# Split weights in padded buffers at set byte distances from the activations, on a two-layer hybrid trunk

## The chip, the cores and the metric

The program runs on one core of a Trainium2 chip. The metric is device time in microseconds, the median of several runs; lower is better. TensorE (PE in the profile; PEld is its weight load), VectorE (DVE), ScalarE (ACT) and GpSimd (POOL) each work through their own instructions in order and wait for each other by semaphores; SyncE (SP) issues most DMAs.

## The reference

A residual stream x of 256 tokens by 2048 passes through two layers in float32. Each layer normalizes x, multiplies it by one wide input matrix, runs two groups of heads, gates them, and multiplies the result by an output matrix that is added to x.

```python
def layer_ab(x, norm_g, w_in, ...):
    h = rms_norm(x, norm_g)
    proj = jnp.einsum('btd,de->bte', h, w_in)
    q, k, v, o_pre, z_a, i_pre, f_pre, z_b, xbc, dt_raw = split_cols(proj, SPLIT_AB)
    y_a = mlstm_branch(...)
    y_b = mamba2_branch(...)
    y = jnp.concatenate([y_a, y_b], axis=-1).astype(x.dtype)
    return x + jnp.einsum('bte,ed->btd', y, w_out)

def layer_cd(x, norm_g, w_in, kv_norm, w_uk, w_uv, ...):
    h = rms_norm(x, norm_g)
    proj = jnp.einsum('btd,de->bte', h, w_in)
    q_c, ckv, z_c, iq, ik, iw, qkv, z_d, b_pre, a_pre = split_cols(proj, SPLIT_CD)
    y_c = dsa_branch(...)
    y_d = gdn_branch(...)
    y = jnp.concatenate([y_c, y_d], axis=-1).astype(x.dtype)
    return x + jnp.einsum('bte,ed->btd', y, w_out)
```

The mixers are an mLSTM, a Mamba-2 SSD, a top-k sparse attention and a gated DeltaNet. Most of the arithmetic lies in the projections by w_in (2048 x 13352 and 2048 x 18064) and w_out (4096 x 2048 and 6144 x 2048).

## The kernel before

**Projections.** float32 is kept by splitting each operand into a high part and a remainder, both of type fp32r, and adding three products: high by high, high by low, low by high. The activations are split once, into hT (the normalized input, 16 blocks of 128 features; each block has 256 columns of high parts and 256 of low parts), into cT (the latent of the sparse attention) and into the units ua, ub and uc (the gated outputs that go into w_out). The weights come by DMA through `load_w` (lines 198 to 212) in groups of 128 x 2048 into wr (three buffers). ScalarE copies wr to wh (the high part, line 210), VectorE subtracts wh from wr to make wl (line 211). wh and wl have two buffers each.

Two helpers use them:

- `proj_tok` (token projection, PSUM tile pt) loads 128 x 128 of the activations into TensorE and moves 512 columns of wh or wl through it.
- `proj_feat` (feature projection, PSUM tile pf) loads 128 x 128 of wh or wl and moves 256 columns of the activations through it.

Every matmul is issued at line 75, transposes at line 79. The order on each engine is set by a scheduler from the order of the code; between the matmuls of a projection, `tick` (line 184) takes one step of the mixers' generators. TensorE's order is the program's.

**Where the tiles lie.** In the built program each tile starts at these bytes of its partition, modulo 256; blocks and column slices inside the tiles are multiples of 512 bytes apart and don't change them:

| tile | start modulo 256 |
|---|---|
| hT | 192 |
| wh, wl (all buffers) | 160 |
| ua, ub, uc | 160 |
| cT | 32 |

So the moving operand's start minus the loaded operand's, modulo 256, is:

| projection | moving | loaded | distance |
|---|---|---|---|
| token, on hT | wh, wl | hT | 224 |
| token, on ua, ub, uc | wh, wl | ua, ub, uc | 0 |
| token, on cT | wh, wl | cT | 128 |
| feature, on hT | hT | wh, wl | 32 |
| feature, on cT | cT | wh, wl | 128 |

**Other places that the change touches.** `tri` (line 103) is a 128 x 256 tile of ones whose left half becomes the upper triangle; `ones` (line 106) is a tile of its own, used in the matmuls den, rbp and gcT. In the gated DeltaNet, `norms` (line 1191) and `delta` (line 1308) square tiles on ScalarE only for the sum of a row (accum_out); the squares themselves go into the scratch tile gjunk. Before that stage the gates of layer cd are computed: 12 token projections in a row, while VectorE steps through a triangular solve (`solve`, U) and GpSimd finishes it (lines 1029 to 1034).

```python
PE.matmul(pts[t][:, :n], hi, wh[:, k % KG, :n], start=k == 0, stop=False)
PE.matmul(pt, wh[:, k, bs], xt[:, i, 0:256], start=g + k == 0 and b % 2 == 0, stop=False)
```

In these two lines, of the token and of the feature projection, the operand named second is loaded and the one named third moves.

Of the kernel before, what the change touches and what calls it, by code (L numbers as in the profile page):

```python
# [8 lines left out]
F32 = mybir.dt.float32  # L9
F32R = mybir.dt.float32r  # L10
I32 = mybir.dt.int32
AF = mybir.ActivationFunctionType
# [15 lines left out]
GONE = -3.4e38  # L28

KG, WR, WS = 4, 3, 2  # L30

STEPS = 1150

# [29 lines left out]
def trunk(ctx, tc, x, rel_bias, ab_norm, ab_w_in, ab_ml_b_i, ab_ml_b_f, ab_ml_norm, ab_ssm_conv_w,  # L63
# [4 lines left out]
    V, A, G = nc.vector, nc.scalar, nc.gpsimd  # L68
    ticking = []

    class PE:
# [5 lines left out]
        @staticmethod  # L77
        def transpose(*args, **kw):
            return held(nc.tensor.transpose(*args, **kw))  # L79
# [9 lines left out]
    cp = ctx.enter_context(tc.tile_pool(name="cp", bufs=1))  # L89
    wp = ctx.enter_context(tc.tile_pool(name="wp", bufs=3))  # L90
# [12 lines left out]
    tri = cp.tile([128, 256], F32, name="tri")  # L103
    V.memset(tri, 1.0)
    G.affine_select(tri[:, 0:128], tri[:, 0:128], pattern=[[1, 128]], compare_op=OP.is_ge, fill=0.0, base=0, channel_multiplier=-1)
    ones = cp.tile([128, 128], F32, name="ones")
    V.memset(ones, 1.0)

    def mx(name):
        return ps.tile([128, 512], F32, name=name, tag="mx")  # L110
# [45 lines left out]
    def pump():  # L156

        for gen in list(bg):
            if next(gen, "end") == "end":
                bg.remove(gen)  # L160
# [11 lines left out]
    def scaled_to(n):  # L172

        while scaling["done"] < n:
            next(scaling["gen"], None)
            scaling["done"] += 1

    def tick():

        if scaling["wait"] is not None and scaling["done"] < 8:  # L180
            scaling["wait"] -= 1
            if scaling["wait"] <= 0:
                scaled_to(scaling["done"] + 1)
                scaling["wait"] = 2
        ticking.append(True)
        if steps and next(steps[0], "end") == "end":
            steps.pop(0)
        ticking.clear()

    def lag(n):  # L190
        for _ in range(n):
            yield
# [2 lines left out]
        while steps:  # L195
            tick()

    def load_w(src, r0, nk, pieces, n):

        pump()  # L200
        shaped = lambda w: w.rearrange("p k n -> p (k n)").rearrange("p (k n) -> p k n", n=n)
        wr = shaped(wp.tile([128, KG, 512], F32, name="wr", tag="wr", bufs=WR))
        if sum(m for _, m, _ in pieces) < n:
            G.memset(wr[:, 0:nk, 0:n], 0.0)
        for c0, m, at in pieces:
            nc.sync.dma_start(wr[:, 0:nk, at:at + m], src[r0:r0 + nk * 128, c0:c0 + m].rearrange("(k p) n -> p k n", p=128))
        wh = shaped(wp.tile([128, KG, 512], F32R, name="wh", tag="wh", bufs=WS))
        wl = shaped(wp.tile([128, KG, 512], F32R, name="wl", tag="wl", bufs=WS))
        with tc.high_priority():
            A.copy(wh[:, 0:nk, 0:n], wr[:, 0:nk, 0:n])  # L210
            V.tensor_tensor(wl[:, 0:nk, 0:n], wr[:, 0:nk, 0:n], wh[:, 0:nk, 0:n].bitcast(F32), op=OP.subtract)  # L211
        return wh, wl

    def proj_tok(src, r0, X, c0, n=512, apart=False):

        pts = [ps.tile([128, 512], F32, name=f"pt{t}", tag="pt") for t in range(2)]
        nk = len(X)

        def part(w, k, t):
            (wh, wl), (xt, i) = w, X[k]  # L220
            hi, lo = xt[:, i, t * 128:t * 128 + 128], xt[:, i, 256 + t * 128:384 + t * 128]
            PE.matmul(pts[t][:, :n], hi, wh[:, k % KG, :n], start=k == 0, stop=False)
            PE.matmul(pts[t][:, :n], hi, wl[:, k % KG, :n], start=False, stop=False)
            PE.matmul(pts[t][:, :n], lo, wh[:, k % KG, :n], start=False, stop=k == nk - 1)

        if apart:

            w = [load_w(src, r0 + g * 128, KG, [(c0, n, 0)], n) for g in range(0, nk, KG)]
            for t in range(2):
                for k in range(nk):  # L230
                    part(w[k // KG], k, t)
                    tick()
            return pts
        for g in range(0, nk, KG):
            w = load_w(src, r0 + g * 128, KG, [(c0, n, 0)], n)
            if g + KG == nk:
                order = [(k, t) for t in range(2) for k in range(KG)]
            else:
                order = [(k, t) for k in range(KG) for t in range(2)]
            for i, (k, t) in enumerate(order):  # L240
                part(w, g + k, t)
                if i % 2:
                    tick()
        return pts

    def proj_feat(src, r0, X, pieces, groups=None, raw=False):

        n = max(p[2] + p[1] for p in pieces)
        n = (n + 127) // 128 * 128
        nb = n // 128  # L250
        pts = [ps.tile([128, 512], F32, name=f"pf{b}", tag="pt") for b in range((nb + 1) // 2)]
        nk = len(X)
        kg = KG * 512 // n
        for g, m in groups or [(g, min(kg, nk - g)) for g in range(0, nk, kg)]:
            wh, wl = load_w(src, r0 + g * 128, m, pieces, n)
            last = g + m == nk
            order = [(k, b) for b in range(nb) for k in range(m)] if last else [(k, b) for k in range(m) for b in range(nb)]
            for at, (k, b) in enumerate(order):
                xt, i = X[g + k]
                if xt is hT and not raw:  # L260
                    scaled_to(i // 2 + 1)
                bs = slice(b * 128, b * 128 + 128)
                pt = pts[b // 2][:, b % 2 * 256:b % 2 * 256 + 256]
                PE.matmul(pt, wh[:, k, bs], xt[:, i, 0:256], start=g + k == 0 and b % 2 == 0, stop=False)
                PE.matmul(pt, wh[:, k, bs], xt[:, i, 256:512], start=False, stop=False)
                PE.matmul(pt, wl[:, k, bs], xt[:, i, 0:256], start=False, stop=last and k == m - 1 and (b % 2 == 1 or b == nb - 1))
                if at % nb == nb - 1:
                    tick()
        return pts
# [164 lines left out]
    with ExitStack() as st:  # L434
        mp = st.enter_context(tc.tile_pool(name="mp", bufs=1))
        np1 = ExitStack()
        X, rb = normed(gab, np1.enter_context(tc.tile_pool(name="np1", bufs=1)), True, 9)
# [48 lines left out]
        pt = mx("RTp")  # L486
# [27 lines left out]
        for i in range(8):  # L514
            k = 1 << i
# [10 lines left out]
        pt = mx("R2Tp")  # L526
# [115 lines left out]
        with tc.tile_pool(name="lp", bufs=1) as lp:  # L642
# [71 lines left out]
            pt = mx("rbp")  # L714
# [10 lines left out]
            for h in range(4):  # L725
# [7 lines left out]
                v = lp.tile([128, 2, 512], F32, name="v", tag="v", bufs=2)  # L733
# [32 lines left out]
    with ExitStack() as st:  # L766
# [3 lines left out]
        X, rb = normed(gcol[:, G_CD:G_CD + 16], kq, False, 6)  # L770
# [185 lines left out]
        pt = mx("rkp")  # L956
# [202 lines left out]
        with tc.tile_pool(name="gp", bufs=1) as gp:  # L1159
# [14 lines left out]
            for i in range(4):  # L1174
                pts = proj_feat(cd_w_in, 0, X, [(CQKV + i * 512, 512, 0)])
                qc = gp.tile([128, 4, 256], F32, name="qc", tag="qc", bufs=QB)
                ssq = gp.tile([128, 2, 4], F32, name="ssq", tag="ssq", bufs=2)
                junk = gp.tile([128, 128], F32, name="gjunk", tag="gjunk")
                for b in range(2):
                    conv_gate(pts[b], gconv, i * 4 + b * 2, 64, None, qc[:, b * 2:b * 2 + 2].rearrange("p b t -> p (b t)"))  # L1180
                rq = gp.tile([128, 8], F32, name="rq", tag="rq", bufs=2)
# [2 lines left out]
                def norms(qc, ssq, rq, rq2):  # L1184
                    yield from lag(LQ)
                    for j in range(4):
                        pt = mx("qt")
                        for t in range(2):
                            transpose(pt[:, t * 128:t * 128 + 128], qc[:, j, t * 128:t * 128 + 128])
                        for t in range(2):  # L1190
                            A.activation(junk, pt[:, t * 128:t * 128 + 128], AF.Square, scale=0.5, accum_out=ssq[:, t, j:j + 1])
                        yield

                    rsqrt(rq, ssq.rearrange("p t j -> p (t j)"), 1.0)
                    V.tensor_scalar(rq, rq, scalar1=0.5 * 128 ** -0.5, scalar2=None, op0=OP.mult)
                    V.tensor_tensor(rq2, rq, rq, op=OP.mult)

                steps.append(norms(qc, ssq, rq, rq2))
                for s in range(2):
                    h0, j0 = i * 8 + s * 4, i * 4 + s * 2  # L1200
# [46 lines left out]
                    o = gp.tile([128, 2, 512], F32, name="og_", tag="og_")  # L1247
                    z = gp.tile([128, 2, 512], F32, name="zg", tag="zg")

                    def delta(s, h0, qc, kT, k0, QD, Wt, vf, o, z, rq, rq2):  # L1250
                        hsl = [slice(h * 128, h * 128 + 128) for h in range(4)]
                        v = gp.tile([128, 2, 512], F32, name="vg", tag="vg")
# [12 lines left out]
                        for c in range(2):  # L1265
# [16 lines left out]
                            u = gp.tile([128, 512], F32, name="u", tag="u")  # L1282
# [22 lines left out]
                        sso = gp.tile([128, 8], F32, name="sso", tag="sso", bufs=2)  # L1305
                        for c in range(2):
                            for h in range(4):
                                A.activation(junk, o[:, c, hsl[h]], AF.Square, accum_out=sso[:, c * 4 + h:c * 4 + h + 1])

                        dup = lambda r: r.rearrange("p (c j) -> p c j", c=2)[:, :, s * 2:s * 2 + 2].unsqueeze(3).to_broadcast([128, 2, 2, 2])  # L1310
                        v4 = lambda r: r.rearrange("p (c j r) -> p c j r", c=2, j=2)
# [87 lines left out]
```

## Time and profile before

| | |
|---|---|
| median of 3 runs | 2129.6 us (2127.21 to 2130.42) |
| profiled execution | 2131.35 us |
| its span, first to last instruction | 2129.6 us |
| TensorE matmul busy | 2091.1 us |
| VectorE busy | 1456.8 us |
| ScalarE busy | 992.4 us |
| GpSimd busy | 115.6 us |
| moved by DMA | 415.16 MB, mean 195 GB/s |
| granted TensorE clock, mean | 0.997 |

The profile is of one execution. A group of instructions has a line, an engine, an operation, the tiles it writes and reads, and a count; "busy" is the time in which at least one of the group ran, and "mean ns of one" is the length of a single one. Matmuls overlap in their pipeline, so the length of one is more than the time from one start to the next; the latter comes from a stretch of time divided by the matmuls in it. The chain of work that ended last is followed back from the last instruction, at each step to what released it.

### The profile page before, as it was taken

The page shows a single profiled execution, that of the slowest core. Times are in us where ns is not written, and L with a number is a line of the kernel's source. Part 1 is how long each engine was busy: PE and PEld are TensorE (multiplying, and loading weights), DVE is VectorE, ACT ScalarE, POOL GpSimd, SP SyncE. Part 2 cuts the span into 40 slices and gives each one's busy share as a digit, 9 for nine tenths or more (in the row PEclk, how much of TensorE's full clock was granted, in tenths as well). Part 3 has the DMA queues.
Part 4 walks back from the last instruction along what each step waited for, and adds up shares of the span by engine and source line. Part 5 has one row for each costly group of instructions (what it writes and reads, how often), then busy time and mean ns, then how long its engine had stood idle before and what let it go on. Part 6 is the DMA issues. An engine that isn't in the chain of part 4 may idle for free.

```text
span 2129.6 us, 31469 instructions
## 1 busy us (share of the span) xinstructions
PE 2091.1 (98%) x12846; PEld 1851.9 (87%) x12846; DVE 1456.8 (68%) x2123; ACT 992.4 (47%) x1311; POOL 115.6 (5%) x145
## 2 busy tenths in 40 slices
PE   7999999999999999999999999999999999999997
PEld 7989997888889788998778888899899999999986
DVE  7998764545454456678879998555676666766765
ACT  5555443334434344456544343455444454444543
POOL 0000020000000000000110002000000001000001
PEclk9999999999999999999999999999999999999999
DMA  6655556655555555576886666755575556566543
GB/s 206 199 193 176 167 179 209 197 179 178 178 178 187 169 194 182 171 246 226 282 238 204 221 207 206 271 184 183 173 227 190 193 174 198 191 196 193 166 166 121
DMA packets 242342, 415.16 MB, mean 195 GB/s; under 512 B 45093, under 2 KB 69206, under 8 KB 240342
## 3 DMA queue, kind: packets, MB, share of 16 engines
q1 hardware_dynamic: 236438, 388.26, 56.0%
q0 software_dynamic: 4912, 23.30, 3.4%
q8 instruction: 101, 1.65, 0.3%
q10 hardware_dynamic: 848, 1.58, 0.2%
q14 instruction: 43, 0.35, 0.0%
HBM read 389.87 MB, written 26.38 MB: 195 GB/s over the span
## 4 chain that ended last, share of the span: by engine, by line
PE 90%; DMA 4%; DVE 4%; ACT 2%; issue 1%; ACTq 0%; SPq 0%
PE pt L75 48%; PE pf L75 32%; DVE wl L211 2%; ACT wh L210 1%; PE py L75 1%; DMA Dt<-gd 1%; PE turn L79 1%; DMA wr<-in_ab_w_in_dram 1%; DMA wr<-in_cd_w_in_dram 1%; PE pog L75 1%; PE pu L75 1%; PE po L75 1%; PE lgt L75 0%; PE num L75 0%; ACT Dt L908 0%
## 5 line engine op out<-in xcount | busy, mean ns | idle before, releaser
L211 DVE TENSOR_TENSOR wl<-wr,wh 128x2048 fp32r<-128x2048 f32 (+1 forms) x337 | 774.0, 2297 | 485.8 <-ACT wh L210 480.2
L210 ACT CAST wh<-wr 128x2048 fp32r<-128x2048 f32 (+1 forms) x337 | 639.8, 1899 | 758.4 <-PE pt L75 433.4
L75 PE MATMUL pf<-hT,wh 128*128 128x256 f32 x4192 | 763.9, 284 | 0.0
L75 PEld LDWEIGHTS pf<-hT,wh 128*128 128x128 f32 x4192 | 645.4, 189 | 6.4 <-issue 3.3
L75 PE MATMUL pt<-wh,hT 128*128 128x512 f32 x1856 | 593.6, 398 | 0.0
L75 PE MATMUL pf<-hT,wl 128*128 128x256 f32 x2096 | 588.0, 281 | 5.0 <-DVE wl L211 5.0
L75 PEld LDWEIGHTS pt<-wh,hT 128*128 128x128 f32 x1856 | 348.8, 188 | 84.3 <-issue 1.9
L75 PEld LDWEIGHTS pf<-hT,wl 128*128 128x128 f32 x2096 | 395.0, 189 | 6.4 <-DVE wl L211 5.8
L75 PE MATMUL pt<-wl,hT 128*128 128x512 f32 x928 | 367.9, 396 | 4.7 <-DVE wl L211 4.7
L75 PE MATMUL pt<-wh,uc 128*128 128x512 f32 x768 | 250.1, 398 | 0.0
L75 PEld LDWEIGHTS pt<-wl,hT 128*128 128x128 f32 x928 | 174.6, 188 | 48.6 <-DVE wl L211 6.3
L75 PEld LDWEIGHTS pt<-wh,uc 128*128 128x128 f32 x768 | 143.7, 188 | 28.6
L75 PE MATMUL pt<-wl,uc 128*128 128x512 f32 x384 | 151.0, 393 | 0.0
L421 DVE SCALAR_TENSOR_TENSOR cy<-pf,gconv,cy 128x255 f32<-128x255 f32 (+2 forms) x192 | 88.2, 477 | 5.6 <-ACT cy L417 3.2
L75 PEld LDWEIGHTS pt<-wl,uc 128*128 128x128 f32 x384 | 72.3, 188 | 13.8 <-DVE wl L211 0.4
L75 PE MATMUL pt<-wh,ua 128*128 128x512 f32 x256 | 80.1, 392 | 0.0
L75 PE MATMUL pt<-wh,ub 128*128 128x512 f32 x256 | 79.1, 389 | 0.0
L390 DVE TENSOR_TENSOR xr<-pt,xr 128x512 f32<-128x512 f32 x80 | 54.9, 686 | 25.4 <-PE pt L75 25.3
L75 PEld LDWEIGHTS pt<-wh,ub 128*128 128x128 f32 x256 | 48.1, 188 | 9.9
L1226 POOL TENSOR_TENSOR QD<-QD,qm 128x256 f32<-128x256 f32 x32 | 30.5, 986 | 474.6 <-DVE qm L1223 241.0
L75 PEld LDWEIGHTS pt<-wh,ua 128*128 128x128 f32 x256 | 47.9, 188 | 9.5
L1019 DVE TENSOR_TENSOR U<-U,tmp 128x62 f32<-128x62 f32 (+30 forms) x62 | 53.1, 857 | 1.2
(457 smaller groups left out, 1802.6 us busy)
## 6 DMA issues: line engine op xcount, KB each, us to landing
wr<-in_cd_w_in_dram SPq DMA_DIRECT2D x140, 1024.0 KB, 5.1
wr<-in_ab_w_in_dram SPq DMA_DIRECT2D x87, 1024.0 KB, 5.1
wr<-in_cd_w_out_dram SPq DMA_DIRECT2D x48, 1024.0 KB, 5.1
wr<-in_ab_w_out_dram SPq DMA_DIRECT2D x32, 1024.0 KB, 5.1
wr<-in_ab_w_in_dram SPq DMA_DIRECT2D x33, 512.0 KB, 4.7
zd<-zk SPq DMA_DIRECT2D x12, 512.0 KB, 5.5
Dt<-gd SPq DMA_DIRECT2D x4, 1024.0 KB, 8.5
Dd<-Dt POOLq DMA_DIRECT2D x4, 1024.0 KB, 6.2
```

The source lines that it names most:

```text
L75: return held(nc.tensor.matmul(*args, **kw))
L79: return held(nc.tensor.transpose(*args, **kw))
L210: A.copy(wh[:, 0:nk, 0:n], wr[:, 0:nk, 0:n])
L211: V.tensor_tensor(wl[:, 0:nk, 0:n], wr[:, 0:nk, 0:n], wh[:, 0:nk, 0:n].bitcast(F32), op=OP.subtract)
L390: V.tensor_tensor(xc, pts[t], xc, op=OP.add)
L421: V.scalar_tensor_tensor(yi[:, s:256], u[:, 0:256 - s], tap(3 - s), yi[:, s:256], op0=OP.mult, op1=OP.add)
L1019: V.tensor_tensor(U[:, 0:s, s + 1:64], U[:, 0:s, s + 1:64], tv, op=OP.subtract)
L1226: G.tensor_tensor(QD[:, h], QD[:, h], qm[:, h // 2 * 256:h // 2 * 256 + 256], op=OP.mult)
```

## The change

The tiles of wh and wl grow by PAD = 64 floats (256 bytes), and `load_w` takes a `shift`, at which the 2048 floats begin inside the tile. The shift is looked up by the first letter of the activation tile's name (hT, cT, or a unit) and by the kind of projection: the first entry is taken in `proj_tok`, the second in `proj_feat`. To make room, `ones` becomes the right half of `tri` (which stays all ones), and gjunk goes: in `norms` the squares overwrite their source in PSUM, and in `delta` they overwrite v, which has been read by then.

```diff
+PAD, SHIFT = 64, {"h": (8, 24), "c": (32, 48), "u": (0, 0)}
...
-    ones = cp.tile([128, 128], F32, name="ones")
-    V.memset(ones, 1.0)
+    ones = tri[:, 128:256]
...
-    def load_w(src, r0, nk, pieces, n):
+    def load_w(src, r0, nk, pieces, n, shift):
...
-        shaped = lambda w: w.rearrange("p k n -> p (k n)").rearrange("p (k n) -> p k n", n=n)
-        wr = shaped(wp.tile([128, KG, 512], F32, name="wr", tag="wr", bufs=WR))
+        shaped = lambda w: w.rearrange("p (k n) -> p k n", n=n)
+        wr = shaped(wp.tile([128, KG * 512], F32, name="wr", tag="wr", bufs=WR))
...
-        wh = shaped(wp.tile([128, KG, 512], F32R, name="wh", tag="wh", bufs=WS))
-        wl = shaped(wp.tile([128, KG, 512], F32R, name="wl", tag="wl", bufs=WS))
+        wh = shaped(wp.tile([128, KG * 512 + PAD], F32R, name="wh", tag="wh", bufs=WS)[:, shift:shift + KG * 512])
+        wl = shaped(wp.tile([128, KG * 512 + PAD], F32R, name="wl", tag="wl", bufs=WS)[:, shift:shift + KG * 512])
...
+        shift = SHIFT[X[0][0].name[0]][0]
...
+        shift = SHIFT[X[0][0].name[0]][1]
...
-                junk = gp.tile([128, 128], F32, name="gjunk", tag="gjunk")
...
-                            A.activation(junk, pt[:, t * 128:t * 128 + 128], AF.Square, scale=0.5, accum_out=ssq[:, t, j:j + 1])
+                            half = pt[:, t * 128:t * 128 + 128]
+                            A.activation(half, half, AF.Square, scale=0.5, accum_out=ssq[:, t, j:j + 1])
...
-                                A.activation(junk, o[:, c, hsl[h]], AF.Square, accum_out=sso[:, c * 4 + h:c * 4 + h + 1])
+                                A.activation(v[:, c, hsl[h]], o[:, c, hsl[h]], AF.Square, accum_out=sso[:, c * 4 + h:c * 4 + h + 1])
```

In the built program hT (192), the units (160), cT (32) and the start of the padded tiles (160) keep their places modulo 256. The split weights inside the tiles move:

| projection | weights at | distance before | distance after |
|---|---|---|---|
| token, on hT | 160 + 32 = 192 | 224 | 0 |
| token, on units | 160 | 0 | 0 |
| token, on cT | 160 + 128, so 32 | 128 | 0 |
| feature, on hT | 160 + 96, so 0 | 32 | 192 |
| feature, on cT | 160 + 192, so 96 | 128 | 192 |

The order of the projections' matmuls, casts and DMAs stays the same nearly everywhere. In the gated DeltaNet the scheduler sets a few rows differently. On ScalarE, in the step of `delta` for the first four heads, this stood before:

```order
L1286 COPY u<-pu 128x512
L1292 COPY og__13463<-pog 128x512
L1308 ACTIVATE gjunk,sso<-og__13463 128x128 x2
L210 CAST wh<-wr 128x2048
L1308 ACTIVATE gjunk,sso<-og__13463 128x128 x2
L210 CAST wh<-wr 128x2048
```

and after the change this stands there (og is the output of the heads, sso the sums):

```order
L1291 COPY u<-pu 128x512
L1297 COPY og__13460<-pog 128x512
L1313 ACTIVATE vg,sso<-og__13460 128x128 x3
L213 CAST wh<-wr 128x2048
L1313 ACTIVATE vg,sso<-og__13460 128x128
L213 CAST wh<-wr 128x2048
```

The squares write v (vg), and one of them has moved ahead of the first cast. On VectorE, in the same stage, where the norms of the queries (rq) are finished beside the scores (qm) of the next heads, this stood before:

```order
L152 SCALAR_TENSOR_TENSOR rq<-nrq,rq 128x8
L211 TENSOR_TENSOR wl<-wr,wh 128x2048
L1195 TENSOR_SCALAR rq<-rq 128x8
L1223 TENSOR_TENSOR qm<-pq,tri 128x512
L1196 TENSOR_TENSOR rq_14462<-rq 128x8
```

and after:

```order
L154 SCALAR_TENSOR_TENSOR rq<-nrq,rq 128x8
L1200 TENSOR_SCALAR rq<-rq 128x8
L1201 TENSOR_TENSOR rq_14458<-rq 128x8
L214 TENSOR_TENSOR wl<-wr,wh 128x2048
L1228 TENSOR_TENSOR qm<-pq,tri 128x512
```

The split wl has moved behind the last two small steps of rq. This occurs three times.

More of the change, by code (lines that the diff above doesn't have):

```diff
@@ L226, in proj_tok @@
         if apart:
-            w = [load_w(src, r0 + g * 128, KG, [(c0, n, 0)], n) for g in range(0, nk, KG)]
+            w = [load_w(src, r0 + g * 128, KG, [(c0, n, 0)], n, shift) for g in range(0, nk, KG)]
             for t in range(2):
@@ L234, in proj_tok @@
         for g in range(0, nk, KG):
-            w = load_w(src, r0 + g * 128, KG, [(c0, n, 0)], n)
+            w = load_w(src, r0 + g * 128, KG, [(c0, n, 0)], n, shift)
             if g + KG == nk:
@@ L252, in proj_feat @@
         nk = len(X)
+        shift = SHIFT[X[0][0].name[0]][1]
         kg = KG * 512 // n
         for g, m in groups or [(g, min(kg, nk - g)) for g in range(0, nk, kg)]:
-            wh, wl = load_w(src, r0 + g * 128, m, pieces, n)
+            wh, wl = load_w(src, r0 + g * 128, m, pieces, n, shift)
             last = g + m == nk
```

## The prediction

> **What bounds the kernel now.** I read the page's busy times first, then the chain of work that ended last by share.
>
> ```profile
> PE 2091.1 (98%) x12846; PEld 1851.9 (87%) x12846; DVE 1456.8 (68%) x2123; ACT 992.4 (47%) x1311; POOL 115.6 (5%) x145
> ...
> PEclk9999999999999999999999999999999999999999
> ...
> PE 90%; DMA 4%; DVE 4%; ACT 2%; issue 1%; ACTq 0%; SPq 0%
> PE pt L75 48%; PE pf L75 32%; DVE wl L211 2%; ACT wh L210 1%; PE py L75 1%; DMA Dt<-gd 1%; PE turn L79 1%; DMA wr<-in_ab_w_in_dram 1%; DMA wr<-in_cd_w_in_dram 1%; PE pog L75 1%; PE pu L75 1%; PE po L75 1%; PE lgt L75 0%; PE num L75 0%; ACT Dt L908 0%
> ```
>
> TensorE is the bound: 98% busy, nine tenths of the chain, at the full granted clock. Two kinds of matmul make four fifths of the chain: pt (token projections: 512 columns of weights move, 128 columns of activations are loaded) and pf (feature projections: 256 columns of activations move, 128 columns of weights are loaded). The change removes none of them, so the only question that matters is how long one takes. For that I read the same chain in order of time (start us, us, what): a stretch of matmuls divided by their count is the time from one start to the next.
>
> ```profile
> 181.06 3.52 PE py L75 x32
> ...
> 768.70 43.32 PE pt L75 x191
> ...
> 859.85 51.81 PE pf L75 x444
> ...
> 1091.35 229.63 PE pt L75 x983
> ```
>
> The stretch at 768.70 gives 226.8 ns for a pt, the one at 1091.35 gives 233.6 ns for the same 512 columns, at 859.85 a pf takes 116.7 ns. The groups of instructions inside those stretches say what differs (columns: count | busy us, mean ns of one | idle before). The windows are 768.9 to 811 us, 1104 to 1147, 861 to 904, and 1349.3 to 1354.7.
>
> ```profile
> L75 PE MATMUL pt<-wh,ua 128*128 128x512 f32 x125 | 38.6, 390 | 0.0
> L75 PE MATMUL pt<-wl,ua 128*128 128x512 f32 x63 | 24.5, 389 | 0.0
> ...
> L75 PE MATMUL pt<-wh,hT 128*128 128x512 f32 x124 | 39.2, 396 | 0.0
> L75 PE MATMUL pt<-wl,hT 128*128 128x512 f32 x62 | 24.5, 396 | 0.0
> ...
> L75 PE MATMUL pf<-hT,wh 128*128 128x256 f32 x248 | 43.4, 279 | 0.0
> L75 PE MATMUL pf<-hT,wl 128*128 128x256 f32 x123 | 34.3, 279 | 0.0
> ...
> L75 PE MATMUL pf<-cT,wh 128*128 128x256 f32 x32 | 5.7, 281 | 0.0
> L75 PE MATMUL pf<-cT,wl 128*128 128x256 f32 x15 | 4.2, 281 | 0.0
> L75 PE MATMUL pf<-hT,wl 128*128 128x256 f32 x1 | 0.3, 281 | 0.0
> ```
>
> The slow and the fast pt have one size, one type and no idle time; a single one lasts 396 against 389 to 390 ns, the same 6 to 7 ns as between starts. What differs is the tile that is loaded: hT, which begins 192 bytes after a multiple of 256, or ua, which begins at 160, as the moving wh and wl do. In bytes modulo 256, moving minus loaded is 224 for the slow pt, 0 for the fast one, 32 for pf on hT and 128 for pf on cT. The last two differ little: the window on cT, with a last pf on hT still in it, has 48 in 5.4 us and the length of one, (5.4 + 0.28) / 48 = 118 ns, against 116.7.
>
> **The change, part by part.**
>
> *Token projections on hT go from 224 to 0.* The counts are in the page's groups:
>
> ```profile
> L75 PE MATMUL pf<-hT,wh 128*128 128x256 f32 x4192 | 763.9, 284 | 0.0
> ...
> L75 PE MATMUL pt<-wh,hT 128*128 128x512 f32 x1856 | 593.6, 398 | 0.0
> L75 PE MATMUL pf<-hT,wl 128*128 128x256 f32 x2096 | 588.0, 281 | 5.0 <-DVE wl L211 5.0
> ...
> L75 PE MATMUL pt<-wl,hT 128*128 128x512 f32 x928 | 367.9, 396 | 4.7 <-DVE wl L211 4.7
> ```
>
> There are 1856 + 928 = 2784 of them. At 233.6 - 226.8 = 6.8 ns each the change saves 18.9 us of TensorE. Its ends are 0 (the tile and not the distance sets the time) and 18.9; I take the upper one, because 0 is a distance that the trace has on the same operation. Projections on ua, ub and uc are at 0 and stay there.
>
> Not all of it arrives. The longest stretch, 983 matmuls from 1091 us, is worth 983 x 6.8 = 6.7 us, and there VectorE runs the triangular solve. Busy time by window (us, PE, PEld, DVE, ACT, POOL, clock, DMA share, GB/s), and what follows it:
>
> ```profile
> 1100.00:1210.00 110.00, 110.00 (x474) 88.55 (x473) 106.77 (x98) 42.32 (x29) 0.00 (x0) 1.00 0.63 207
> 1210.00:1320.00 110.00, 110.00 (x473) 88.59 (x472) 106.81 (x97) 42.76 (x30) 2.33 (x1) 1.00 0.65 214
> ...
> 1317.67 6.05 POOL L1029 TENSOR_SCALAR_AFFINE_SELECT U<-U 128x4096 f32<-128x4096 f32 x1 [246.90 <-DVE U L1027]
> ...
> 1326.89 7.55 POOL L1033 COPY Uw<-U 64x4096 f32<-64x4096 f32 x1
> ...
> 1328.45 10.20 DVE L211 TENSOR_TENSOR wl<-wr,wh 128x2048 fp32r<-128x2048 f32 x2 [1.99 <-ACT wh L210]
> ...
> 1336.50 0.39 PE L75 MATMUL pf<-hT,wl 128*128 128x256 f32 x1 [4.09 <-DVE wl L211]
> ```
>
> VectorE is busy 213.6 of 220 us and has 6.4 us to spare, about what TensorE would gain. When the solve ends, GpSimd copies for 7.55 us, the split wl beside it takes until about 1336.5, and TensorE waits 4.09 us. If the solve doesn't end sooner, a faster TensorE only waits longer there. Queued behind each wl on VectorE are the solve's steps, and the matmuls wait for wl, so either engine can be the late one. Between 0 and 6.7 us I take half, 3.4. On the other 18.9 - 6.7 = 12.2 us I count the 90% that TensorE has of the chain, 11.0. Token projections: **14.4 us**.
>
> *Feature projections on hT go from 32 to 192*, 4192 + 2096 = 6288 of them, and no stream of this kernel is at 192 in a matmul of this kind. Bound from both sides: in the chain's row for py, 32 matmuls with only 64 moving columns take 3.52 us, 110 ns each, so loading 128 columns does not go faster and a pf cannot come under 110. Upwards I allow the whole spread that pt shows, 116.7 + 6.8 = 123.5. That is -6.7 to +6.8 ns, in time 6288 x 6.7 x 0.9 = 38 us either way. The nearest hints are single matmuls that stream while another tile's weights load (start us, us):
>
> ```profile
> 1387.07 0.28 PE L75 MATMUL pf<-hT,wl 128*128 128x256 f32 x1
> 1387.18 0.38 PE L75 MATMUL po<-vd,PT 128*128 128x128 f32 x2
> ...
> 1669.76 0.28 PE L75 MATMUL pf<-hT,wl 128*128 128x256 f32 x1
> 1669.89 0.48 PE L75 MATMUL pks<-S,kT 128*128 128x256 f32 x1
> ```
>
> PT lies at distance 0 from hT and the next start comes after 0.11 us; kT lies at 96 and it comes after 0.13. So pf too depends on distance; the multiple of 64 is the better of the two here, and pt's best is 0. The moving operand of 192 is a multiple of 64 where the present 32 is not. On that I take a bit over a third of the way to the floor, 2.5 ns (114.2 ns), 6288 x 2.5 x 0.9 = **14.1 us**. This is the weakest step of the sum: pf on cT, at 128, is also a multiple of 64 and is 118, not 114. The few projections on cT go to the same distances, and I leave them out.
>
> *The rest costs nothing that I can see.* The rows for it:
>
> ```profile
> L107 DVE MEMSET ones<- x1: 165/165/165, 1.2 to 1.2; 128x128 f32 x1
> ...
> L1191 ACT ACTIVATE gjunk<-qt x32: 256/277/278, 1569.2 to 1979.5; 128x128 f32<-128x128 f32 x32
> L1308 ACT ACTIVATE gjunk<-og__13463 x8: 307/312/313, 1609.0 to 1627.6; 128x128 f32<-128x128 f32 x8
> ```
>
> The memset of 0.17 us ran while TensorE waited for its first data. The 32 squares that now write into PSUM and the 64 that write into v keep their count; if writing there costs or saves 0.1 us each (a third of one, an estimate), it is up to 10 us of ScalarE in a stage of some 490 us, on an engine that is 47% busy; without that cover a cast of wh comes later, and the matmuls on it. Writing v waits for nothing new, since the matmuls that read v feed the values that are squared. In the reordered VectorE rows three wl go behind two small steps each, under 1 us in all. No DMA is added or moved past another; weights are asked for about 1% faster of queues that have 4% of the chain.
>
> The sum: 14.4 + 14.1 = 28.5 us off the profiled execution's span of 2129.6 us. That execution took 2131.35 us with what lies around the span; the median of the three runs is 2129.6, so 28.5 less is **2101 us**.
>
> **A rule against the change.** The Trainium skill, page "TensorE: Matmul & The Clock Gate", section "Step-by-step: what each phase is for", says that TensorE has two separate read ports into SBUF and that loading the next tile's weights takes no read bandwidth from the running matmul. By it no distance could matter and the sum would be 0, the second rival below; the 396 against 389 to 390 ns of one operation speak against the rule as it stands. The same page's section "Back-to-back issue gap" gives a warm spacing of N / 2.4 + 2.5 ns, 109 ns for 256 columns; by it the floor of pf would be 109 instead of 110, and the best case 6 us lower.
>
> **The rivals.**
>
> *Distance 192 is a bad one for pf.* The worst distance that pt shows is 224, and 192 is its neighbour, where 32 is a neighbour of the good 0. From a pf of 116.7 + 14.4 / (6288 x 0.9) us, that is 119.2 ns, the loss eats the token projections' gain; at 120.5 to 123.5 ns the kernel takes 2137 to 2154 us. For it: cT's 118. Against it: kT's single case of 0.13 us is at 96, no multiple of 64.
>
> *The distance isn't what sets the time.* Then hT is slow because it is hT (its own place in SBUF, which stays at 192), nothing moves, and the time is 2129.6 us. For it: in the steady stretches the tile and the distance always change together. Against it: with hT as the moving operand the trace shows different times for different loaded tiles.
>
> *pf stays within 1 ns of what it is.* Only the token projections count: 14.4 us and up to 6 us either way, 2109 to 2121 us, middle 2115. For it: pf at 32 and 128 differ by little.
>
> **How the numbers follow.** The forecast (pf under 115.7 ns, 2074 to 2109 us, likeliest 2101) gets 0.55, pf as it is 0.25, pf slower 0.13, no effect 0.07. The range runs from 2077, near the floor, to 2130, which takes in no effect; beyond it lies most of the slower rival. A measurement of this kernel tells a difference of about 0.2%, 4.3 us. Faster by more: the first two cases and a little of the slower pf, 0.81. Same: 0.08. Slower: 0.11.
>
> **What would show it.** Right: one pt on hT at 389 to 390 ns instead of 396, the stretch of 983 under 227 us; one pf under 277 ns and under 115 between starts; VectorE over 98% busy beside the solve and the wait at its end over 4.09 us. Wrong: pt on hT still at 396 (no effect of distance), or one pf at 281 ns or more (192 is bad). A busy ScalarE ahead of late casts in the last stage would show that the squares are not free.

## The result, and the profile after

The changed kernel takes 2108.3 us in the median of four runs (2105.77 to 2113.91), the kernel before 2130.01 us beside it (four runs, 2127.21 to 2134.18). The ratio is 0.990, with a 95% interval from 0.9874 to 0.9926: faster by 1.0%, 21.7 us where 28.5 were forecast. The profiled execution took 2105.77 us, the lowest of the four; its span fell from 2129.6 to 2103.9 us, by 25.7.

The first view is the page of the changed kernel: busy times, the chain of work by engine, and the four costly groups (count | busy us, mean ns of one | idle before, what ended it). L78 is now the line of the matmuls, L213 that of the cast wh, L214 that of the split wl.

```profile
PE 2060.9 (98%) x12846; PEld 1836.4 (87%) x12846; DVE 1457.4 (69%) x2122; ACT 987.4 (47%) x1311; POOL 115.6 (5%) x145
...
PE 87%; DVE 5%; DMA 4%; ACT 3%; issue 1%; ACTq 0%; SPq 0%
...
L78 PE MATMUL pf<-hT,wh 128*128 128x256 f32 x4192 | 751.0, 282 | 0.0
...
L78 PE MATMUL pf<-hT,wl 128*128 128x256 f32 x2096 | 585.0, 279 | 5.6 <-DVE wl L214 5.6
L78 PE MATMUL pt<-wh,hT 128*128 128x512 f32 x1856 | 582.1, 392 | 0.3 <-ACT wh L213 0.3
...
L78 PE MATMUL pt<-wl,hT 128*128 128x512 f32 x928 | 362.3, 390 | 5.7 <-DVE wl L214 5.7
```

TensorE's matmuls are the same 12846, and they take 2091.1 - 2060.9 = 30.2 us less. Every one of the four groups is shorter: a pt on hT by 6 ns (398 to 392, 396 to 390), a pf by 2 (284 to 282, 281 to 279). But span less busy time grew from 38.5 to 43.0 us, and the share of VectorE in the chain from 4 to 5%: 4.5 of the 30.2 us came back as time in which TensorE has nothing to run. That is one execution, and the fastest of the four.

The chain of the changed kernel in order of time (start us, us, what) has the two stretches from which the forecast took its numbers.

```profile
849.46 50.34 PE pf L78 x444
...
1077.40 223.18 PE pt L78 x983
```

223.18 / 983 = 227.0 ns for a pt on hT where 233.6 stood, and 50.34 / 444 = 113.4 ns for a pf where 116.7 stood. Whether the stretch of 983 pays depends on VectorE beside it. Its windows (us, then busy us of PE, PEld, DVE, ACT, POOL, clock, DMA share, GB/s):

```profile
1100.00:1210.00 110.00, 110.00 (x487) 91.05 (x486) 108.97 (x91) 44.88 (x31) 0.00 (x0) 1.00 0.67 220
1210.00:1300.00 90.00, 90.00 (x399) 74.53 (x398) 88.90 (x84) 35.63 (x26) 1.83 (x1) 1.00 0.66 216
```

VectorE is busy for 197.87 of these 200 us, 99%, where it had 97%. The chain around the end of the solve, first before the change:

```profile
1324.95 1.53 PE pf L75 x13
...
1326.50 1.92 ACT wh L210
...
1328.45 8.01 DVE wl L211
...
1336.50 13.57 PE pf L75 x100
```

and after it:

```profile
1300.58 5.55 PE pf L78 x47
...
1306.15 1.92 ACT wh L213
...
1308.09 8.81 DVE wl L214
...
1316.95 13.07 PE pf L78 x99
```

From the start of the 983 matmuls to the pf behind the late wl it was 1336.50 - 1091.35 = 245.15 us and is 1316.95 - 1077.40 = 239.55. So 5.6 of the 6.45 us that TensorE gained in the stretch arrived; 0.8 went into a wl that took 8.81 instead of 8.01 us.

### The profile page after: what moved, and what is told of

Its sections match the earlier page's. It is cut to its first block, busy times and chain, and to the rows that moved or that the text cites. A ratio compares the mean times of both kernels' runs of the same rounds, so it can differ in the third digit from the quotient of the medians.

```text
span 2103.9 us, 31457 instructions
## 1 busy us (share of the span) xinstructions
PE 2060.9 (98%) x12846; PEld 1836.4 (87%) x12846; DVE 1457.4 (69%) x2122; ACT 987.4 (47%) x1311; POOL 115.6 (5%) x145
## 4 chain that ended last, share of the span: by engine, by line
PE 87%; DVE 5%; DMA 4%; ACT 3%; issue 1%; ACTq 0%; SPq 0%
PE pt L78 47%; PE pf L78 31%; DVE wl L214 3%; ACT wh L213 2%; PE py L78 1%; PE turn L82 1%; DMA Dt<-gd 1%; DMA wr<-in_ab_w_in_dram 1%; DMA wr<-in_cd_w_in_dram 1%; PE pu L78 1%; ACT Dt L913 1%; PE pog L78 1%; PE po L78 1%; PE lgt L78 0%; PE num L78 0%
## 5 line engine op out<-in xcount | busy, mean ns | idle before, releaser
L214 DVE TENSOR_TENSOR wl<-wr,wh 128x2048 fp32r<-128x2048 f32 (+1 forms) x337 | 775.9, 2303 | 463.2 <-ACT wh L213 458.2
L213 ACT CAST wh<-wr 128x2048 fp32r<-128x2048 f32 (+1 forms) x337 | 639.7, 1898 | 742.5 <-PE pt L78 426.8
L78 PE MATMUL pf<-hT,wh 128*128 128x256 f32 x4192 | 751.0, 282 | 0.0
L78 PEld LDWEIGHTS pf<-hT,wh 128*128 128x128 f32 x4192 | 641.5, 189 | 6.3 <-issue 3.3
L78 PE MATMUL pf<-hT,wl 128*128 128x256 f32 x2096 | 585.0, 279 | 5.6 <-DVE wl L214 5.6
L78 PE MATMUL pt<-wh,hT 128*128 128x512 f32 x1856 | 582.1, 392 | 0.3 <-ACT wh L213 0.3
L78 PEld LDWEIGHTS pt<-wh,hT 128*128 128x128 f32 x1856 | 348.2, 188 | 74.0 <-issue 1.9
L78 PEld LDWEIGHTS pf<-hT,wl 128*128 128x128 f32 x2096 | 395.8, 189 | 7.3 <-DVE wl L214 6.5
L78 PE MATMUL pt<-wl,hT 128*128 128x512 f32 x928 | 362.3, 390 | 5.7 <-DVE wl L214 5.7
L78 PE MATMUL pt<-wh,uc 128*128 128x512 f32 x768 | 250.6, 398 | 0.0
L78 PEld LDWEIGHTS pt<-wl,hT 128*128 128x128 f32 x928 | 174.3, 188 | 43.9 <-DVE wl L214 7.2
L78 PEld LDWEIGHTS pt<-wh,uc 128*128 128x128 f32 x768 | 143.7, 188 | 28.4
L78 PE MATMUL pt<-wl,uc 128*128 128x512 f32 x384 | 150.7, 392 | 0.0
L78 PEld LDWEIGHTS pt<-wl,uc 128*128 128x128 f32 x384 | 72.3, 188 | 14.0 <-DVE wl L214 0.4
L78 PE MATMUL pt<-wh,ua 128*128 128x512 f32 x256 | 80.1, 392 | 0.0
L78 PE MATMUL pt<-wh,ub 128*128 128x512 f32 x256 | 79.1, 389 | 0.0
L78 PEld LDWEIGHTS pt<-wh,ub 128*128 128x128 f32 x256 | 48.1, 188 | 10.0
L78 PEld LDWEIGHTS pt<-wh,ua 128*128 128x128 f32 x256 | 47.9, 188 | 9.5
```

Of the source, the lines that this page charges most:

```text
L78: return held(nc.tensor.matmul(*args, **kw))
```

## The experiments

The distances are those of the table in the section on the change: moving minus loaded start, modulo 256 bytes. "Steady" below is the mean time from one matmul's start to the next in the trace, without the gaps in which TensorE waits (over 150 ns for pf, 260 for pt).

### One half of the change at a time

The edits are against the changed kernel, here and in all that follows.

```diff
-PAD, SHIFT = 64, {"h": (8, 24), "c": (32, 48), "u": (0, 0)}
+PAD, SHIFT = 64, {"h": (8, 0), "c": (32, 0), "u": (0, 0)}
```

> The change with only the token projections moved (hT from 224 to 0, cT from 128 to 0); the feature projections stay at 32 and 128. Theory (the distance sets each matmul's time, and the parts add): one pt on hT 390 ns, a long stretch 226.8 ns from start to start, features as before; 14 to 17 us under the kernel before, about 2115. Rival (hT's own place sets it): 396 ns, 2130.

```diff
+PAD, SHIFT = 64, {"h": (0, 24), "c": (0, 48), "u": (0, 0)}
```

> The change with only the feature projections moved (hT from 32 to 192, cT from 128 to 192); token projections stay at 224 and 128. Theory: 7 to 11 us under the kernel before, about 2121; pf has the two lasting spacings of the changed kernel, 113.3 and 117.8 ns. Rival (the gain comes from elsewhere, features give nothing): 2130.

```diff
+PAD, SHIFT = 64, {"h": (0, 0), "c": (0, 0), "u": (0, 0)}
```

> The change with every shift at 0: longer buffers, shared ones, no scratch tile, distances as before. Theory: the rest of the change costs nothing, within 3 us of 2130. Rival (the rest costs 4 to 8 us, which is why less than the forecast arrived): 2134 to 2138.

All three ran beside 15 runs of the kernel before (median 2128.98 us). Span and busy times are from the profile's pages:

| kernel | median us | ratio (95%) | span | TensorE busy | rest |
|---|---|---|---|---|---|
| neither shifted | 2130.09 (11 runs) | 1.0002 (0.9993 to 1.0011) | 2127.4 | 2090.0 | 37.4 |
| token projections only | 2116.86 (5) | 0.9944 (0.9932 to 0.9957) | 2115.1 | 2075.0 | 40.1 |
| feature projections only | 2120.41 (5) | 0.9954 (0.9941 to 0.9968) | 2118.7 | 2078.8 | 39.9 |

The chain rows of the kernel with the token projections shifted alone, then of the one with the feature projections alone:

```profile
850.99 51.81 PE pf L78 x444
...
1080.48 223.18 PE pt L78 x983
```

```profile
855.52 50.35 PE pf L78 x444
...
1086.51 229.63 PE pt L78 x983
```

Each half moves its own stretch and leaves the other where it was. Longer buffers, the shared `ones`, the squares without gjunk and the reordered rows cost nothing that eleven runs can show (the interval reaches 0.1% either way). The halves take 12.1 and 8.6 us off the median; together 20.7, and the whole change has 21.7. The token half gave less than the 14 to 17 us expected of it. Against the kernel with neither, the token half takes 15.0 us off TensorE's busy time, of which 12.3 reach the span, and the feature half 11.2, of which 8.7 do. About four fifths of the busy time arrive in both. Measured by the matmuls' own spacing it is less: the steady matmuls on hT add up to 17.2 us less in the token half (638.9 to 621.7 us), those of all features to 12.6 us less in the feature half, so that about seven tenths reach the span. These are single executions; where the rest went was not followed.

### Is it the distance, or the tile?

A sweep, in which every call of a projection takes the next of eight distances; a letter in the name of its PSUM tile says which (a is 0, b is 32, up to h at 224).

```diff
+FEAT, TOK = [0, 32, 64, 96, 128, 160, 192, 224], [0, 32, 64, 96, 128, 160, 192, 224]
...
+    at = START[tile[0]] - 160
+    return (at - dists[i] if kind == "f" else at + dists[i]) % 256 // 4, "abcdefgh"[i]
...
-        pts = [ps.tile([128, 512], F32, name=f"pt{t}", tag="pt") for t in range(2)]
+        shift, code = turn_of("t", X[0][0].name)
+        pts = [ps.tile([128, 512], F32, name=f"pt{code}{t}", tag="pt") for t in range(2)]
```

> The changed kernel, but each projection call takes the next of eight distances, 0 to 224 in steps of 32 bytes, on every activation tile; the PSUM tiles carry a letter, a for 0 to h for 224. Theory: the mean length of one pt depends on the letter and not on the tile, hT and units alike, about 390 ns at a and 396 at h; pf differs by letter, g (192) near 276 to 281, b (32) near 279. If 192 is the best, no letter lies below g; a rival is that another distance holds the short spacing alone. Time between 2105 and 2135.

One run, 2143.49 us, over the 2105 to 2135 expected. Its chain runs through all eight distances on the same tile hT, 96 matmuls each, beside the solve:

```profile
1103.49 22.41 PE ptd L89 x96
1125.90 22.40 PE pte L89 x96
1148.30 22.48 PE ptf L89 x96
1170.78 22.39 PE ptg L89 x96
1193.17 22.39 PE pth L89 x96
1215.56 21.77 PE pta L89 x96
1237.33 22.40 PE ptb L89 x96
1259.73 21.98 PE ptc L89 x96
```

21.77 / 96 = 226.8 ns at 0 and 229.0 at 64; the other six lie between 233.2 and 234.2. Same operation, same loaded tile, same engines beside it: what is left is where the weights lie. hT starts 32 bytes after the units, so at one distance the weights lie at another place modulo 256 for hT than for the units. The units give the same steady value at each distance within 0.3 ns, except 1 ns more at 0. So it is the distance that sets the time, neither the tile nor the weights' own place. For the features the sweep gave, steady on hT, 119.8 ns at 0, 116.8 at 32, 117.3 at 64, 119.9 at 96, 118.8 at 128, 118.2 at 160, 115.5 at 192 and 118.3 at 224. The change had picked the best of the eight for both.

The counterpart puts the units, which were at 0 before and after, at 224:

```diff
+PAD, SHIFT = 64, {"h": (8, 24), "c": (32, 48), "u": (56, 0)}
```

> The changed kernel with one thing more: the token projections on the units ua, ub, uc, at 0 in both kernels, go to 224. Theory (distance, whatever the tile): one pt on ub goes from 389 to 395 or 396 ns, 227 to 233 from start to start; 1920 matmuls x 6.6 ns x 0.9 = 11 us more than the changed kernel, about 2119. Rival (the tile sets it): ub stays at 389, the time at 2108.

```profile
760.07 44.56 PE pt L78 x191
```

This stretch on a unit took 43.32 us before: 44.56 / 191 = 233.3 ns, what hT had had. The time was 2113.31 us (ratio to the kernel before 0.9928, interval 0.9910 to 0.9945), so about 5 us slower than the changed kernel's 2108.3, or 6 by the ratios to the kernel before, and not the 11 expected. All the units' steady matmuls together took 428.7 instead of 418.0 us, so the cost is on TensorE; only about half of it reached the end, and why was not followed.

### How fine is the pattern?

The same sweep in steps of 4 bytes around the two chosen distances:

```diff
+FEAT, TOK = [192, 196, 200, 204, 208, 176, 180, 184], [0, 4, 8, 12, 16, 240, 244, 248]
```

> As the sweep, in steps of 4 bytes: features at 192, 196, 200, 204, 208, 176, 180, 184 (letters a to h), tokens at 0, 4, 8, 12, 16, 240, 244, 248. Theory: only multiples of 16 or 32 matter, so a to d are alike (features 113.3 or 117.8 ns, tokens 227) and e and f differ from them. Rival: some finer distance keeps the features at 113.3 throughout, or takes tokens under 226.5; then 2108 can be beaten. Time 2105 to 2130.

One run, 2138.68 us, over the 2105 to 2130 expected. The chain rows of tokens at 0, 4, 12 and 244 bytes (a, b, d, g):

```profile
1164.83 23.03 PE ptg L89 x96
...
1210.13 21.80 PE pta L89 x96
1231.93 22.81 PE ptb L89 x96
...
1277.14 21.98 PE ptd L89 x96
```

227.1 ns at 0 becomes 237.6 at 4, 229.0 at 12 and 239.9 at 244, more than at any distance of the coarse sweep. The theory that only multiples of 16 or 32 matter fell: single words of 4 bytes count. All the activation tiles start at multiples of 32 bytes, so within 32 bytes the distance and the weights' own start change together, and the sweeps by 4 bytes can't tell which of the two counts. For features, steady, 192 had 115.0, 196 119.5, 200 118.5, 204 114.4, 208 118.8, 176 118.9, 180 114.1, 184 118.4.

A third sweep filled in distances in between:

```diff
+FEAT, TOK = [180, 52, 116, 244, 20, 12, 76, 140], [0, 12, 28, 44, 60, 76, 140, 204]
```

> Distances that the two sweeps left out: features call by call at 180, 52, 116, 244, 20, 12, 76, 140, token projections at 0, 12, 28, 44, 60, 76, 140, 204. One look, read by the steady time from start to start at each distance, not by the total time. Theory A, the good distances repeat by 64 bytes (180 and 204 are as good as 192 or better, 0 is the good one for tokens and 64 comes next): features at 52, 116 and 244 come out near the 114.1 ns of 180, at 12, 76 and 140 near the 114.4 ns of 204, and tokens at 60, 76, 140 and 204 lie together within 1 ns. Theory B, the pattern is one of the whole 256 bytes: 180 again gives 113.3 to 114.5 ns, the others scatter between 116 and 120 ns, and for tokens none of the new distances comes under 228 ns. Total time between 2125 and 2145 us by both.

One run, 2128.11 us. Features, in that order: 114.3, 118.8, 117.8, 116.8, 119.5, 119.7, 116.5, 119.1 ns; tokens 227.2, 229.0, 227.8, 230.0, 227.8, 228.9, 231.1, 231.1. So the pattern does not repeat by 64 bytes (theory A fell): 180 stays good on other calls, 52, 116 and 244 are not. Theory B held but for tokens at 28 and 60, which came just under its 228. Nothing beat 0 for tokens.

### Which matmul pays?

wh stays at 192 (features) and 0 (tokens), wl alone goes to 96 and 224:

```diff
+APART = {8: 0, 24: 48}
...
-        wl = shaped(wp.tile([128, KG * 512 + PAD], F32R, name="wl", tag="wl", bufs=WS)[:, shift:shift + KG * 512])
+        wl = shaped(wp.tile([128, KG * 512 + PAD], F32R, name="wl", tag="wl", bufs=WS)[:, APART.get(shift, shift):APART.get(shift, shift) + KG * 512])
```

> The changed kernel, but wl alone lies elsewhere in projections on hT: tokens 224 instead of 0, features 96 instead of 192; wh stays. If a matmul is slowed by the weight load that runs beside it, which is that of the next matmul, then in features the matmul with wh just ahead of one with wl is the slow one, and the one with wl is not; if by its own load, the one with wl is. In tokens the one that moves wl is the slow one either way. About a third of the difference to the bad distances: 6 us for tokens and 8 for features, 2118 to 2126.

One run, 2129.49 us, slower than expected. In the features two matmuls on wh are followed by one on wl. The groups of one window, 865 to 905 us, of this kernel (count | busy us, mean ns of one | idle before):

```profile
L79 PE MATMUL pf<-hT,wh 128*128 128x256 f32 x228 | 40.3, 281 | 0.0
L79 PE MATMUL pf<-hT,wl 128*128 128x256 f32 x114 | 31.8, 279 | 0.0
```

In the changed kernel's own window, 855 to 895 us, both had 276:

```profile
L78 PE MATMUL pf<-hT,wh 128*128 128x256 f32 x238 | 40.5, 276 | 0.0
L78 PE MATMUL pf<-hT,wl 128*128 128x256 f32 x118 | 32.6, 276 | 0.0
```

The group that was not moved became the longer one. Which load runs beside which matmul shows in the timeline (start us, us, what), first the matmuls, then the load of wl:

```profile
870.07 0.40 PE L79 MATMUL pf<-hT,wh 128*128 128x256 f32 x2
870.31 0.28 PE L79 MATMUL pf<-hT,wl 128*128 128x256 f32 x1
```

```profile
870.19 0.19 PEld L79 LDWEIGHTS pf<-hT,wl 128*128 128x128 f32 x1
```

The load of wl starts 0.12 us ahead of the matmul on wl, with the second wh. From start to start, over all features of the kernel, the steady wh matmul ahead of a wl takes 122.7 ns, the wh ahead of a wh 114.8, the wl itself 116.2; in the changed kernel all three lie between 114.6 and 114.9. The one that pays most is the matmul that is streaming while wl's block is loaded for the next. That fits a collision of the two reads, which no run shows directly. In the token projections, where the split weights move, wl itself is the slow one, at 233.4; but a wh ahead of a wh has 232.0 there although neither moved, a wh ahead of a wl only 228.4, and that stays open.

### Two lasting spacings

The changed kernel ran again beside one with features at 180 bytes:

```diff
+PAD, SHIFT = 64, {"h": (8, 27), "c": (32, 51), "u": (0, 0)}
```

> The changed kernel as it is, on the same chip as the kernel with features at 180, so that the two are compared without a change of chip between them. Expected 2106 to 2114 us; features on hT in a mixture of the spacings 113.3 and 117.8 ns with a mean near 115, tokens at 226.8 ns.

> The changed kernel with one distance altered: features at 180 bytes instead of 192 (on hT and on cT), token projections at 0 as in the changed kernel. Theory: features have two lasting spacings, 113.3 and 117.8 ns, and the distance sets how often the matmuls fall into the first; at 180 they nearly always do, steady mean about 114.1 against 115.0 ns, so 0.9 ns x 6288 x 0.9 = 5 us less than the changed kernel at most, 2103 to 2106 us. Rival: the 180 of the sweep stood on one call only, in one place, and other calls fall into the slow spacing as at 192; then 2107 to 2112 us, no difference from the changed kernel.

The same stretch of 444 features, in the chain of the changed kernel's second profile, then of the one with 180:

```profile
847.32 52.30 PE pf L78 x444
```

```profile
846.27 50.37 PE pf L78 x444
```

52.30 / 444 = 117.8 ns, where the first profile of this very kernel had 113.4. Apart from its first matmuls, a stretch at 192 keeps one spacing or the other to its end, in all but one of the 225 stretches of 12 or more in the two profiles, and a new stretch falls into either. Of the matmuls in such stretches, 75% lay in stretches with the short spacing (a mean under 115.5 ns) in the first profile of the changed kernel and 68% in the second; with 180 it was 93%. The kernel with 180 took 2103.03 us, the changed one 2108.47 beside it. One of its four runs, 2107.71, lay among the other's, so it ran again on another chip, with the neighbour 204 beside it:

```diff
+PAD, SHIFT = 64, {"h": (8, 21), "c": (32, 45), "u": (0, 0)}
```

> The changed kernel with features at 204 bytes in place of 192 (on hT and cT), token projections at 0. In the sweep by 4 bytes every long stretch at 204 ran at 113.6 to 114.4 ns. Theory, the share of matmuls in the lasting spacing of 113.3 ns sets what the features cost: nearly all of them are in it here, so the time is that of 180, 2102 to 2105 us, some 5 us under the changed kernel's 2108. Rival, 180 won by its place in that one comparison: then 204 gives 2107 to 2111 us.

> Features at 180 bytes again, on another chip or another time, since one of its four executions (2107.71 us) lay among those of the changed kernel. Theory: 2101 to 2106 us, a median at least 3 us under 2108. Rival: no difference, 2107 to 2110 us.

180 took 2105.26 us (ratio to the kernel before 0.9885, interval 0.9868 to 0.9901), 204 2106.67 (0.9889, 0.9874 to 0.9903). On this second chip no changed kernel ran beside them. All eight runs at 180 have a median of 2103.8 us (2101.97 to 2107.71), all eight of the changed kernel 2108.5 (2105.77 to 2113.91): 4.7 us less, and 180 is the lower in 59 of the 64 pairs. It is the best version that ran, though its second profile has 89% of the matmuls in the short spacing. 204 missed its expectation: 82% had the short spacing, but the long one reached 120.1 ns in one stretch, the steady mean on hT was 115.2 ns, no better than the 114.8 and 115.2 of the two profiles at 192, and its time lies between the two, told apart from neither. What a few calls of a sweep show is not yet the mean over a kernel.

## Why the prediction was right, and where its sizes were off

**TensorE as the bound:** right. Its busy time fell by 30.2 us and the span by 25.7. In the second profile of the changed kernel it was 25.0 (2091.1 to 2066.1) and 22.1 us, with more of the features in the long spacing.

**The distance as the cause:** right. The sweep separates it from the tile, the units at 224 reproduce hT's old 233.3 ns, and the rival of no effect is out. With it goes the forecast of no effect by the rule of the Trainium skill (page "TensorE: Matmul & The Clock Gate", section "Step-by-step: what each phase is for") that a weight load takes no read bandwidth from a running matmul: here the same matmul takes from 226.8 to 239.9 ns with the place of its operands.

**Token projections, 14.4 us:** measured 12.1. The 6.8 ns came from two stretches; over all steady matmuls on hT it was 6.2 (233.3 to 227.1 ns), and TensorE saved 15.0 us instead of 18.9. In the solve stretch I let half arrive and it was 5.6 of 6.45 us, also in the token half alone. After the change the end of the solve on GpSimd stands here (start us, us, what):

```profile
1298.17 6.05 POOL L1034 TENSOR_SCALAR_AFFINE_SELECT U<-U 128x4096 f32<-128x4096 f32 x1 [241.42 <-DVE U L1032]
```

That is 220.8 us behind the start of the stretch, where it was 226.3: the solve ended 5.5 us sooner, nearly as much as TensorE gained. The wl beside GpSimd's copy began 6.4 us sooner and took 0.8 longer. So on the other projections 6.5 us arrived where 11.0 were forecast: two errors of opposite sign, and the sum looks better than its parts.

**Feature projections, 14.1 us:** measured 8.6. This is the mis-sized term, the one called the weakest. 2.5 ns x 6288 = 15.7 us of TensorE were forecast, and the feature half saved 11.2, steady 117.0 to 115.0 ns. The 114.2 ns is a value at which hardly any stretch stays: 192 gives 113.3 or 117.8 by stretches, and the mean follows the share of each. The groups of the page after the change show the smaller mean too: 2 ns. Of what TensorE saved, 78% arrived in that execution and not 90; the 90 was TensorE's share of the chain before, and with a faster TensorE that share is itself only 87%.

**The reason for a gain at 192:** wrong, and the sign right by luck. The sum took 192 for a good distance as a multiple of 64, with a pf that came 0.11 us before the next start beside a load at distance 0 and 0.13 at 96. In the sweep the other multiples of 64 (0, 64 and 128 bytes) gave 119.8, 117.3 and 118.8 ns, all slower than the 116.8 of 32, and 0 is as slow as 96 (119.9). The trace before spoke against it already, in its token projections on cT, at 128 (window 1355.1 to 1360.6 us):

```profile
L75 PE MATMUL pt<-wh,cT 128*128 128x512 f32 x16 | 5.2, 394 | 0.0
```

Their steady spacing is 232.1 ns, near the 233.3 of 224 and not the 227 of 0. No run shows a rule from which 192 could have been foretold; here only the sweep found it.

**The rest at nothing:** right, a ratio of 1.0002 with neither shifted. cT, left out, gained 0.8 us (118.5 to 114.2 ns on 185 matmuls).

**The rivals:** 192 as a bad distance for pf was wrong by its sign, but six of the eight distances in the coarse sweep are worse than the 116.8 to 117 of 32, so the risk was real. pf within 1 ns of what it was (2109 to 2121 us) gave a range whose edge lies by the measured time, though its mechanism did not occur: pf moved by 2 ns. The 2074 us at which the case of the forecast begins does not follow from the sum, which gives 2077 at the floor of 110 ns; the shortest pf spacing that any stretch kept was 113.3.

**What would show it:** pt at 390 to 392 over all, within 2 ns of what was said, and the stretch of 983 in 223.18 us, under 227; pf under 115 between starts and at 276 ns in the first profile's stretch, but 282 and 279 over all, not under 277. VectorE was 99% busy beside the solve. The wait of pf for wl at the end of the solve was to exceed 4.09 us; the longest is 4.6 (waits of the changed kernel: what waits, for what, us in total, times, longest):

```profile
PE pf L78 <- DVE wl L214: 5.6, 3, 4.6
```

What stays open: where each of the 4.5 us of new idle time lies. The named waits on wl and wh grew from 9.7 to 11.6 us, and the rest is in gaps too small to be followed. Nor is it known why single words matter, or what decides into which spacing a stretch falls.

## What to carry to other kernels

Where TensorE is the bound and a kernel is short of nothing else, compare matmuls of one shape by the place of their operands: start addresses of the moving and the loaded operand, in steps of 4 bytes, are a free parameter. Between the best and the worst distance lay 5% of a matmul here; the change itself gained 2.7% on the token and 1.7% on the feature projections. Find the distance by a sweep inside one kernel, not by a rule, and then time the whole kernel, since a stretch can hold one of two spacings. Take the expected gain from the mean spacing over all matmuls of a group, and count three tenths of it as not arriving until shown otherwise.

## What the runs showed of the hardware

- A matmul of 512 columns (fp32r) took from 226.8 ns at distance 0 to 239.9 at 244; one of 256 columns from 113.3 to 120, with the order of the work unchanged.
- The pattern has a grain of 4 bytes and no period of 64: tokens 227.1 at 0, 237.6 at 4, 229.0 at 12.
- Features at 192 bytes hold 113.3 or 117.8 ns for a whole stretch (444 matmuls in 50.34 or 52.30 us, the same kernel twice).
- With wl's block apart, the matmul running beside its load paid most (122.7 ns against 114.8 and 116.2).
